# Two-part norms of a decoder stack: first products on four weight blocks, started inside the norm's first part

## The chip, the cores and the metric

One core of one Trainium2 chip runs the whole program. The metric is the device time of one execution in microseconds (us): the median of three runs, beside one more execution that was profiled.

Names used below: PE is TensorE (matrix products), DVE is VectorE, ACT is ScalarE, POOL is GpSimd, SP is SyncE, whose queue issues the weight loads. A norm here is an RMS norm. Everything is fp32; each operand of a large product is kept as a high part (h) and a rest (l), and a product is made of three: wh·xh, wh·xl and wl·xh.

## The reference, cut to what matters

Two stacks follow each other on 512 positions of width 1024, kept transposed as 8 tiles x[0..7] of 128 features by 512 positions. The first stack is two layers with norms ahead of each part. The second has two layers, each a mixer (an even one with attention and a state space, an odd one with a gated recurrence) and a feed-forward network, with a norm behind each part as well as ahead of it:

```
x = x + rmsnorm(mixer(rmsnorm(x, pre)), post)
x = x + rmsnorm(swiglu(rmsnorm(x, pre2)), post2)
swiglu(a) = (silu(a @ w_gate) * (a @ w_up)) @ w_down
```

So three times in the second stack a part ends with a norm behind it (a post norm, whose result is added to x) and the next norm ahead starts at once from the new x: even mixer to feed-forward network, feed-forward network to odd mixer, odd mixer to feed-forward network. The fourth post norm ends in the store of the output.

## The kernel before, in words

**Weights.** `plan` (L166) holds the list of all weight blocks in the order of use. `fill(n)` (L170) loads blocks ahead until n are waiting: a load into one of 3 `raw` buffers by SP's queue (L179), then wh on ACT (L181), then wl on DVE (L182), into 3 buffers each. `weights` (L185) fills to three and hands out the oldest. A full block is 128 by 1024 elements, 512 KB.

**Products.** `dense` (L200) makes a 128 by 512 output tile of one block: per 128 rows k three matmuls of 512 columns (L196 to L198). It can be told to do one half of the columns (`HALVES`, two slices of 256). `dense_first` (L209) is used for the first blocks behind a norm: it takes several blocks at once and makes first, for every k, wh·xh and wl·xh of each block (L218, L219), then wh·xl (L223), so that work on the first tiles can begin before the last are there. Behind a two-part norm it does so for columns 0 to 255 and then for 256 to 511.

**The two-part norm.** `PostNorm.last` (L1253) computes the last one or two output tiles of a part in two halves of the columns. The mean of squares is a product with a matrix of ones (L1251), of the sum of the earlier tiles' squares (`acc`, added up on POOL, L1237) and of each last tile's squares. Callbacks wait in `late` and are run by `flush` at given places in the last products. `finish(c)` (L1274) then makes rstd for the half (L239 to L242, two ACT and two DVE operations) and for each k scales y (L1279), subtracts it from x (L1280), and makes xn[k] h on ACT (`head`, L257); behind these come xn[k] l on DVE (`rest`, L261). After the second half `norm_square` (L264) squares each x tile on ACT and adds them on POOL (a copy for the first, L270, then 7 adds, L272); their sum feeds one product with the ones (L279) that gives the next norm's rstd, which is multiplied in only behind the products.

**Where it is used.** In the feed-forward networks behind a two-part norm, `dense_first` takes blocks 0 and 1 in halves, and blocks 2 and 3 follow as whole products (L307 to L309). In the odd mixer it takes blocks 0 to 2 in halves (L1851); block 3 follows as a whole one. The odd mixer goes on with a short convolution on DVE (`conv`, L1806), gates (`gates`, L1819) that need its split result (L532, L534), and further blocks named gb and xb.

**PSUM.** Each phase opens a pool of the 8 banks (`psums`, L147): in a feed-forward network 6 for products (`mm`) and 2 others, in the mixers 2 and 6, in the odd mixer 5 and 3. A phase's pool is given back at its end; the next phase's tiles wait for the old ones in the same bank.

**Order.** The program is written in one sequence; a planner then places each instruction on its engine's queue by its own estimate of when operands are ready, so neighbours on an engine can change places. Each engine then works its queue in order.

Of the kernel before, what the change touches and what calls it, by code (L numbers as in the profile page):

```python
# [9 lines left out]
F32 = mybir.dt.float32  # L10
FR = mybir.dt.float32r
# [7 lines left out]
S = 512  # L19
# [42 lines left out]
class Model:  # L62
    def __init__(self, tc, ap, ctx):
        self.tc, self.nc, self.ap, self.ctx = tc, tc.nc, ap, ctx
        nc = self.nc
        self.per = ctx.enter_context(tc.tile_pool(name="per", bufs=1))
        lead = self.per.tile([128, LEAD], F32, name="lead")
        nc.gpsimd.memset(lead, 0.0)
        self.act = ctx.enter_context(tc.tile_pool(name="act", bufs=1))
        self.wp = ctx.enter_context(tc.tile_pool(name="wp", bufs=1))  # L70
        self.tmp = ctx.enter_context(tc.tile_pool(name="tmp", bufs=2))
        self.dram = ctx.enter_context(tc.tile_pool(name="dram", bufs=1, space=bass.MemoryType.DRAM))
        self.x = []
# [72 lines left out]
    @contextmanager  # L146
    def psums(self, **bufs):  # L147

        with self.tc.tile_pool(name="ps", bufs=1, space=bass.MemoryType.PSUM, reuse_waits="tile") as p:
            self.ps, self.ps_bufs = p, bufs  # L150
            yield

    def psum(self, name, tag="px"):
        return self.ps.tile([128, S], F32, name=name, tag=tag, bufs=self.ps_bufs[tag])

# [14 lines left out]
    def fill(self, n):  # L170

        nc = self.nc
        while len(self.loaded) < n and self.todo:
# [5 lines left out]
            nc.sync.dma_start(raw, flat)  # L179
            h, l = (self.wp.tile([128, cols], FR, name=n, tag=n, bufs=3) for n in ("wh", "wl"))  # L180
            nc.scalar.activation(h, raw, AF.Copy)  # L181
# [18 lines left out]
    def dense(self, out, w, k0, nk, x, kt, c=slice(0, S), done=0):  # L200
# [3 lines left out]
        for k in range(done, nk):  # L204
            s = slice(k * 128, (k + 1) * 128)
            xh, xl = x[k0 + k]
            self.mm3(out[:, c], (h[:, s], l[:, s]), (xh[:, c], xl[:, c]), k0 + k == 0, k0 + k == kt - 1)

    def dense_first(self, srcs, name, parts):  # L209

        t = self.nc.tensor
        outs = [self.psum_mm(name) for w in srcs]
        ws = [self.weights(w) for w in srcs]
        for c in parts:
            for k in range(KD):
                s = slice(k * 128, (k + 1) * 128)
                for o, (h, l) in zip(outs, ws):
                    t.matmul(o[:, c], lhsT=h[:, s], rhs=self.xn[k][0][:, c], start=(k == 0), stop=False)  # L218
                    t.matmul(o[:, c], lhsT=l[:, s], rhs=self.xn[k][0][:, c], start=False, stop=False)  # L219
            for o, (h, l) in zip(outs, ws):  # L220
                for k in range(KD):
                    s = slice(k * 128, (k + 1) * 128)
                    t.matmul(o[:, c], lhsT=h[:, s], rhs=self.xn[k][1][:, c], start=False, stop=(k == KD - 1))  # L223
        return outs
# [38 lines left out]

    def norm_square(self, k):  # L264
        nc = self.nc
        sq = self.sq()
        nc.scalar.activation(sq, self.x[k], AF.Square)  # L267
        if self.sq_acc is None:
            self.sq_acc = self.tmp.tile([128, S], F32, name="sqacc", tag="sqacc", bufs=1)
            nc.gpsimd.tensor_copy(self.sq_acc, sq)  # L270
        else:
            nc.gpsimd.tensor_tensor(self.sq_acc, self.sq_acc, sq, op=ALU.add)  # L272

# [10 lines left out]
    def ffn(self, wgu, wd, out_tile, begin=None, side=None, pn=None):  # L284
# [3 lines left out]
        with tc.tile_pool(name="ffn", bufs=1, reuse_waits="tile") as hp, self.psums(mm=6, px=2):  # L288
# [7 lines left out]
            if pn:  # L296
                ready = self.dense_first([gu(i) for i in range(2)], "gu", HALVES)
            side = side(hp) if side else iter(())
# [7 lines left out]

            if pn:  # L307
                for i in (2, 3):
                    ready.append(gate_up(i))  # L309
            for m in range(KF):  # L310
# [35 lines left out]
LOOKAHEAD = 2  # L346
NRAW = 3
PARTS = ((0, 8), (8, 7), (15, 7))
HALVES = (slice(0, S // 2), slice(S // 2, S))
# [870 lines left out]
class PostNorm:  # L1220
# [32 lines left out]
    def last(self, tiles, x, kt):  # L1253
# [31 lines left out]
class NextNorm:  # L1285


    def __init__(self, M, gain):
# [17 lines left out]
class Store:  # L1306


    def __init__(self, M, out):
# [462 lines left out]
class Odd(Phase2):  # L1772
# [13 lines left out]
    def run(self, pn):  # L1786
        M, nc, tc = self.M, self.nc, self.tc
        act, tt, ts, stt = nc.scalar.activation, nc.vector.tensor_tensor, nc.vector.tensor_scalar, nc.vector.scalar_tensor_tensor
        with ExitStack() as st:
# [60 lines left out]

            ready = M.dense_first([self.ap["od_in"][i] for i in range(3)], "xb", HALVES)  # L1851
            conv(0)
# [85 lines left out]
```

## Time and profile before

| | |
|---|---|
| median of 3 runs | 3290.86 us (3290.36 to 3291.94) |
| the profiled execution's own time | 3292.49 us |
| its span, first to last instruction | 3290.7 us |
| mean granted TensorE clock | 0.991 |
| PE busy | 3200.9 us, 97% of the span |
| DVE, ACT, POOL busy | 1732.0, 1319.8, 187.2 us |
| even mixer to feed-forward network (called A) | about 2325 to 2385 us of the span |
| feed-forward network to odd mixer (B) | about 2708 to 2761 us |
| odd mixer to feed-forward network (C) | about 2885 to 2938 us |

How to read it: matmuls are pipelined, so the duration of one says less than the distance from its start to the next one's. The clock's two levels are 2.4 GHz (granted clock 1.0) and 1.2 GHz.

### The profile page before, as it was taken

The page shows a single profiled execution, that of the slowest core. Times are in us where ns is not written, and L with a number is a line of the kernel's source. Part 1 is how long each engine was busy: PE and PEld are TensorE (multiplying, and loading weights), DVE is VectorE, ACT ScalarE, POOL GpSimd, SP SyncE. Part 2 cuts the span into 40 slices and gives each one's busy share as a digit, 9 for nine tenths or more (in the row PEclk, how much of TensorE's full clock was granted, in tenths as well). Part 3 has the DMA queues.
Part 4 walks back from the last instruction along what each step waited for, and adds up shares of the span by engine and source line. Part 5 has one row for each costly group of instructions (what it writes and reads, how often), then busy time and mean ns, then how long its engine had stood idle before and what let it go on. Part 6 is the DMA issues. An engine that isn't in the chain of part 4 may idle for free.

```text
span 3290.7 us, 38872 instructions
## 1 busy us (share of the span) xinstructions
PE 3200.9 (97%) x15174; PEld 2566.7 (78%) x15178; DVE 1732.0 (53%) x2767; ACT 1319.8 (40%) x2041; POOL 187.2 (6%) x184
## 2 busy tenths in 40 slices
PE   8999999999999999999999999998999999989998
PEld 6888856788888888875778888876788887778887
DVE  5443468664433444357774443687554428664433
ACT  4232346743323332243763322355533227643322
POOL 1000100010000000010010000000200011010000
PEclk9999999999999999999999999999999999999999
DMA  4333341033333332343113333322233332323332
GB/s 158 111 97 97 108 128 61 26 107 100 97 94 100 96 96 93 100 126 98 49 62 96 96 93 100 113 79 58 93 96 96 93 100 71 102 71 96 97 95 79
DMA packets 114473, 306.65 MB, mean 93 GB/s; under 512 B 21840, under 2 KB 35056, under 8 KB 114288
## 3 DMA queue, kind: packets, MB, share of 16 engines
q1 hardware_dynamic: 114288, 304.16, 29.9%
q8 instruction: 119, 1.95, 0.2%
q14 instruction: 66, 0.54, 0.0%
HBM read 292.18 MB, written 10.09 MB: 92 GB/s over the span
## 4 chain that ended last, share of the span: by engine, by line
PE 86%; DVE 6%; ACT 4%; DMA 3%; issue 1%; SPq 0%; POOL 0%; DVEq 0%; ACTq 0%; POOLq 0%
PE gu L196 14%; PE gu L197 14%; PE gu L198 14%; PE o L197 8%; PE o L198 8%; PE o L196 8%; DMA conv<-hp_d 1%; PE conv L962 1%; PE wo L197 1%; PE wo L196 1%; PE wo L198 1%; PE lgD L1080 1%; PE v L196 1%; DVE wl L182 0%; PE v L197 0%
## 5 line engine op out<-in xcount | busy, mean ns | idle before, releaser
L181 ACT ACTIVATE wh<-raw 128x1024 fp32r<-128x1024 f32 (+2 forms) x550 | 550.3, 1001 | 1492.9 <-PE gu L197 843.0
L182 DVE TENSOR_TENSOR wl<-raw,wh 128x1024 fp32r<-128x1024 f32 (+2 forms) x550 | 633.0, 1151 | 547.3 <-ACT wh L181 542.7
L196 PE MATMUL o<-hid,wh 128*128 128x512 f32 (+1 forms) x1100 | 419.2, 381 | 0.0
L197 PE MATMUL o<-hid,wh 128*128 128x512 f32 (+1 forms) x1100 | 418.9, 381 | 0.0
L198 PE MATMUL o<-hid,wl 128*128 128x512 f32 (+1 forms) x1100 | 418.5, 380 | 0.0
L315 DVE SCALAR_TENSOR_TENSOR us<-gu,rstd 128x512 f32<-128x512 f32 x132 | 91.2, 691 | 400.7 <-PE gu L198 400.7
L196 PEld LDWEIGHTS o<-hid,wh 128*128 128x128 f32 x1100 | 206.8, 188 | 39.9
L197 PEld LDWEIGHTS o<-hid,wh 128*128 128x128 f32 x1100 | 206.8, 188 | 39.8
L198 PEld LDWEIGHTS o<-hid,wl 128*128 128x128 f32 x1100 | 206.8, 188 | 39.1
L313 DVE SCALAR_TENSOR_TENSOR gs<-gu,rstd 128x512 f32<-128x512 f32 x132 | 91.3, 692 | 259.3 <-PE gu L198 258.5
L272 POOL TENSOR_TENSOR sqacc<-sqacc,sq 128x512 f32<-128x512 f32 x70 | 104.2, 1488 | 369.4 <-ACT sq L267 367.4
L318 ACT ACTIVATE hid<-gs 128x512 fp32r<-128x512 f32 x132 | 83.5, 632 | 93.1 <-DVE gs L316 93.1
L196 PE MATMUL gu<-xn0h,wh 128*128 128x512 f32 x258 | 103.3, 400 | 0.0
L197 PE MATMUL gu<-xn6l,wh 128*128 128x512 f32 x258 | 100.6, 390 | 1.9 <-DVE xn6l L261 1.9
L197 PE MATMUL gu<-xn0l,wh 128*128 128x512 f32 x258 | 100.9, 391 | 0.0
L198 PE MATMUL gu<-xn0h,wl 128*128 128x512 f32 x258 | 100.9, 391 | 0.0
L198 PE MATMUL gu<-xn1h,wl 128*128 128x512 f32 x258 | 100.9, 391 | 0.0
L197 PE MATMUL gu<-xn1l,wh 128*128 128x512 f32 x258 | 100.9, 391 | 0.0
L197 PE MATMUL gu<-xn2l,wh 128*128 128x512 f32 x258 | 100.9, 391 | 0.0
L196 PE MATMUL gu<-xn1h,wh 128*128 128x512 f32 x258 | 100.9, 391 | 0.0
L196 PE MATMUL gu<-xn2h,wh 128*128 128x512 f32 x258 | 100.8, 391 | 0.0
L198 PE MATMUL gu<-xn2h,wl 128*128 128x512 f32 x258 | 100.7, 390 | 0.0
(1386 smaller groups left out, 7069.9 us busy)
## 6 DMA issues: line engine op xcount, KB each, us to landing
raw<-in_ffn_gu SPq DMA_DIRECT2D x176, 512.0 KB
raw<-in_f_gu SPq DMA_DIRECT2D x88, 512.0 KB
raw<-in_ffn_d SPq DMA_DIRECT2D x64, 448.0 KB
raw<-in_w_in SPq DMA_DIRECT2D x36, 512.0 KB
raw<-in_ffn_d SPq DMA_DIRECT2D x32, 512.0 KB
raw<-in_f_d SPq DMA_DIRECT2D x32, 448.0 KB
raw<-in_w_out SPq DMA_DIRECT2D x32, 256.0 KB
raw<-in_f_d SPq DMA_DIRECT2D x16, 512.0 KB
```

The lines of the kernel that those rows point to most:

```text
L181: nc.scalar.activation(h, raw, AF.Copy)
L182: nc.vector.tensor_tensor(l, raw, h.bitcast(F32), op=ALU.subtract)
L196: t.matmul(out, lhsT=wh, rhs=xh, start=first, stop=False)
L197: t.matmul(out, lhsT=wh, rhs=xl, start=False, stop=False)
L198: t.matmul(out, lhsT=wl, rhs=xh, start=False, stop=last)
L272: nc.gpsimd.tensor_tensor(self.sq_acc, self.sq_acc, sq, op=ALU.add)
L313: nc.vector.scalar_tensor_tensor(gs, g, -1.0, self.nrstd, op0=ALU.mult, op1=ALU.mult)
L315: nc.vector.scalar_tensor_tensor(us, u, -1.0, self.nrstd, op0=ALU.mult, op1=ALU.mult)
L318: nc.scalar.activation(h, gs, AF.Copy)
L962: nc.tensor.matmul(p[32 * g:32 * g + 32], lhsT=cw[:, g, k], rhs=st[:, g, 4 * k:4 * k + S], start=(k == 0), stop=(k == 7))
L1080: nc.tensor.matmul(lg[:, :C], lhsT=self.dq[h][:, q], rhs=self.dk[h][:, :C], start=True, stop=False)
```

## The change

Four edits go together.

- Two PSUM banks (`pp`) belong to no phase. In every phase they stand for two of the phase's mm banks, in rotation with the others, which begin with the third.
- `start_next`, called by `PostNorm.last` where another norm follows (three times, not at the store): behind the last product of the old part, the first blocks' wh·xh and wl·xh of columns 0 to 255 for k 0 to 3, for two blocks, into the two banks; then the flush that finishes the second half of the norm; then k 4 to 7.
- `dense_first` takes over what was started, and does four blocks in halves in all three places; wh and wl have 4 buffers each.
- The first half's xl (`rest`) is written behind the second half's rstd; the squares' sum starts on ACT directly, and the 7 adds behind a two-part norm go to DVE in place of POOL. With two last tiles, the first flush comes one tile later.

```diff
+        self.pp = ctx.enter_context(tc.tile_pool(name="pp", bufs=1, space=bass.MemoryType.PSUM, reuse_waits="tile"))
...
     def psum(self, name, tag="px"):
+        if tag == "mm":
+            self.turn = (self.turn + 1) % self.ps_bufs["mm"]
+            if self.turn < PP:
+                return self.pp.tile([128, S], F32, name=name, tag="pp", bufs=PP)
+            return self.ps.tile([128, S], F32, name=name, tag=tag, bufs=self.ps_bufs[tag] - PP)
...
-            h, l = (self.wp.tile([128, cols], FR, name=n, tag=n, bufs=3) for n in ("wh", "wl"))
+            h, l = (self.wp.tile([128, cols], FR, name=n, tag=n, bufs=NW2) for n in ("wh", "wl"))
...
+    def start_next(self, between):
+        self.fill(1 + LOOKAHEAD)
+        got = []
+        for i in range(2):
+            got.append(self.loaded.popleft())
+            self.fill(1 + LOOKAHEAD)
+        ws = [w for _, w in got]
+        outs = [self.pp.tile([128, S], F32, name="first", tag="pp", bufs=PP) for w in ws]
+        self.heads_first(outs, ws, HALVES[0], range(0, 4))
+        between()
+        self.heads_first(outs, ws, HALVES[0], range(4, KD))
+        self.started = outs, ws, [k for k, _ in got]
...
         for c in parts:
-            for k in range(KD):
-                s = slice(k * 128, (k + 1) * 128)
-                for o, (h, l) in zip(outs, ws):
-                    t.matmul(o[:, c], lhsT=h[:, s], rhs=self.xn[k][0][:, c], start=(k == 0), stop=False)
-                    t.matmul(o[:, c], lhsT=l[:, s], rhs=self.xn[k][0][:, c], start=False, stop=False)
+            if c.start or not n:
+                self.heads_first(outs, ws, c)
+            else:
+                self.heads_first(outs[n:], ws[n:], c)
...
-    def norm_square(self, k):
+    def norm_square(self, k, eng=None):
         nc = self.nc
+        if self.sq_acc is None:
+            self.sq_acc = self.tmp.tile([128, S], F32, name="sqacc", tag="sqacc", bufs=1)
+            nc.scalar.activation(self.sq_acc, self.x[k], AF.Square)
+            return
         sq = self.sq()
         nc.scalar.activation(sq, self.x[k], AF.Square)
-        if self.sq_acc is None:
-            self.sq_acc = self.tmp.tile([128, S], F32, name="sqacc", tag="sqacc", bufs=1)
-            nc.gpsimd.tensor_copy(self.sq_acc, sq)
-        else:
-            nc.gpsimd.tensor_tensor(self.sq_acc, self.sq_acc, sq, op=ALU.add)
+        (eng or nc.gpsimd).tensor_tensor(self.sq_acc, self.sq_acc, sq, op=ALU.add)
...
-                ready = self.dense_first([gu(i) for i in range(2)], "gu", HALVES)
+                ready = self.dense_first([gu(i) for i in range(4)], "gu", HALVES)
...
-                    if i == (len(parts) - 1 if c.start == 0 else 0):
+                    if c.start and i == 0 or c.start == 0 and m == KD - 1 and i == len(parts) - 1:
                         self.flush()
...
-        self.flush()
+        if self.next.follows:
+            self.M.start_next(self.flush)
+        else:
+            self.flush()
...
         r = M.rstd_of(self.ms[:, c])
+        if c.start:
+            self.next.rest(HALVES[0])
         for k in range(KD):
...
-        self.next.rest(c)
+        if c.start:
+            self.next.rest(c)
...
-                self.M.norm_square(k)
+                self.M.norm_square(k, self.M.nc.vector)
...
-            ready = M.dense_first([self.ap["od_in"][i] for i in range(3)], "xb", HALVES)
+            ready = M.dense_first([self.ap["od_in"][i] for i in range(4)], "xb", HALVES)
```

`PP` is 2 and `NW2` is 4. A scratch region for descriptors is halved to 1024 bytes.

## Rows read from the trace of the kernel before

**Rows 1.** The page: busy time of the engines over the whole span.

```profile
PE 3200.9 (97%) x15174; PEld 2566.7 (78%) x15178; DVE 1732.0 (53%) x2767; ACT 1319.8 (40%) x2041; POOL 187.2 (6%) x184
```

**Rows 2.** Stretches: length, busy of PE, PEld, DVE, ACT, POOL, clock, DMA share, GB/s.

```profile
2348.50:2385.30 36.80, 30.00 (x148) 24.01 (x147) 28.19 (x49) 16.11 (x32) 12.60 (x8) 0.86 0.20 70
2726.70:2760.50 33.80, 27.97 (x174) 24.95 (x174) 29.96 (x53) 20.40 (x34) 12.74 (x10) 0.90 0.25 82
2900.50:2937.80 37.30, 29.35 (x149) 24.62 (x148) 28.20 (x49) 16.16 (x31) 12.62 (x8) 0.86 0.21 69
2775.00:2815.00 40.00, 40.00 (x178) 33.12 (x177) 39.88 (x57) 38.11 (x50) 0.20 (x2) 1.00 0.36 113
```

**Rows 3.** Timeline of PE, neighbours in B and C: start, duration, what (idle before, and its releaser).

```profile
2729.79 0.28 PE L218 MATMUL xb<-xn0h,wh 128*128 128x256 f32 x1
2729.91 0.28 PE L219 MATMUL xb<-xn0h,wl 128*128 128x256 f32 x1
...
2907.20 0.41 PE L218 MATMUL gu<-xn2h,wh 128*128 128x256 f32 x1
2907.41 0.41 PE L219 MATMUL gu<-xn2h,wl 128*128 128x256 f32 x1
...
2935.04 0.39 PE L196 MATMUL gu<-xn4h,wh 128*128 128x512 f32 x1
2935.26 0.39 PE L197 MATMUL gu<-xn4l,wh 128*128 128x512 f32 x1
```

**Rows 4.** Timeline of PE around C: matmuls that waited.

```profile
2888.53 0.70 PE L1251 MATMUL ms<-sqacc,ones 128*128 128x256 f32 x2 [1.27 <-POOL sqacc L1237]
...
2902.79 0.70 PE L1251 MATMUL ms<-sq,ones 128*128 128x256 f32 x2 [2.10 <-ACT sq L1231]
...
2905.75 0.58 PE L218 MATMUL gu<-xn0h,wh 128*128 128x256 f32 x1 [2.03 <-DVE sq L241]
...
2919.75 0.38 PE L223 MATMUL gu<-xn3l,wh 128*128 128x256 f32 x1 [0.91 <-DVE xn3l L261]
```

**Rows 5.** Timelines of ACT, DVE and POOL around C.

```profile
2899.54 0.51 ACT L257 ACTIVATE xn0h<-x,vecs 128x256 fp32r<-128x256 f32 x1 [1.27 <-DVE x L1280]
...
2905.40 0.49 ACT L257 ACTIVATE xn7h<-x,vecs 128x256 fp32r<-128x256 f32 x1
...
2906.01 0.48 DVE L261 SCALAR_TENSOR_TENSOR xn1l<-x,vecs,xn1h 128x256 fp32r<-128x256 f32 x1
...
2909.23 0.76 DVE L1279 TENSOR_TENSOR pn<-pn,rstd 128x256 f32<-128x256 f32 x2
...
2915.24 9.84 POOL L272 TENSOR_TENSOR sqacc<-sqacc,sq 128x512 f32<-128x512 f32 x7
...
2918.21 1.49 DVE L261 SCALAR_TENSOR_TENSOR xn3l<-x,vecs,xn3h 128x256 fp32r<-128x256 f32 x1
...
2943.17 0.69 DVE L316 TENSOR_TENSOR gs<-gs,us 128x512 f32<-128x512 f32 x1
```

**Rows 6.** Timelines of ACT and DVE: the weight splits behind C's first products.

```profile
2926.04 2.00 ACT L181 ACTIVATE wh<-raw 128x1024 fp32r<-128x1024 f32 x2 [3.12 <-PE gu L223]
...
2933.38 1.23 DVE L182 TENSOR_TENSOR wl<-raw,wh 128x1024 fp32r<-128x1024 f32 x1 [3.89 <-ACT wh L181]
```

**Rows 7.** Timeline of PE in B: the mean, the ones product, the block behind it.

```profile
2729.02 0.70 PE L1251 MATMUL ms<-sq,ones 128*128 128x256 f32 x2 [2.10 <-ACT sq L1231]
...
2753.26 1.91 PE L279 MATMUL ms<-sqacc,ones 128*128 128x512 f32 x2
2754.18 1.27 PE L196 MATMUL xb<-xn0h,wh 128*128 128x512 f32 x1
...
2760.53 0.39 PE L196 MATMUL gb<-xn0h,wh 128*128 128x512 f32 x1
```

**Rows 8.** The odd mixer's last gates: DVE's split and PE's first gate product.

```profile
2814.10 0.69 DVE L534 TENSOR_TENSOR sl<-xc,sh 128x512 fp32r<-128x512 f32 x1
...
2816.00 0.39 PE L196 MATMUL gate<-sh,wh 128*128 128x512 f32 x1
```

More of the change, by code (lines that the diff above doesn't have):

```diff
@@ L72, in __init__ @@
         self.dram = ctx.enter_context(tc.tile_pool(name="dram", bufs=1, space=bass.MemoryType.DRAM))
+        self.pp = ctx.enter_context(tc.tile_pool(name="pp", bufs=1, space=bass.MemoryType.PSUM, reuse_waits="tile"))
+        self.turn = 0
+        self.started = None
         self.x = []
@@ L149, in psums @@
         with self.tc.tile_pool(name="ps", bufs=1, space=bass.MemoryType.PSUM, reuse_waits="tile") as p:
-            self.ps, self.ps_bufs = p, bufs
+            self.ps, self.ps_bufs, self.turn = p, bufs, 1
             yield
     def psum(self, name, tag="px"):
+        if tag == "mm":
[3 more added lines that the diff above has]
+            return self.ps.tile([128, S], F32, name=name, tag=tag, bufs=self.ps_bufs[tag] - PP)
         return self.ps.tile([128, S], F32, name=name, tag=tag, bufs=self.ps_bufs[tag])
@@ L207, in dense, with heads_first @@
             self.mm3(out[:, c], (h[:, s], l[:, s]), (xh[:, c], xl[:, c]), k0 + k == 0, k0 + k == kt - 1)
+    def heads_first(self, outs, ws, c, ks=range(KD)):
+        t = self.nc.tensor
+        for k in ks:
+            s = slice(k * 128, (k + 1) * 128)
+            for o, (h, l) in zip(outs, ws):
+                t.matmul(o[:, c], lhsT=h[:, s], rhs=self.xn[k][0][:, c], start=(k == 0), stop=False)
+                t.matmul(o[:, c], lhsT=l[:, s], rhs=self.xn[k][0][:, c], start=False, stop=False)
+    def start_next(self, between):
[10 more added lines that the diff above has]
+        self.started = outs, ws, [k for k, _ in got]
     def dense_first(self, srcs, name, parts):
         t = self.nc.tensor
-        outs = [self.psum_mm(name) for w in srcs]
-        ws = [self.weights(w) for w in srcs]
-        for c in parts:
-            for k in range(KD):
-                s = slice(k * 128, (k + 1) * 128)
-                for o, (h, l) in zip(outs, ws):
-                    t.matmul(o[:, c], lhsT=h[:, s], rhs=self.xn[k][0][:, c], start=(k == 0), stop=False)
-                    t.matmul(o[:, c], lhsT=l[:, s], rhs=self.xn[k][0][:, c], start=False, stop=False)
+        outs, ws, n = [], [], 0
+        if self.started:
+            outs, ws, keys = self.started
+            n, self.started = len(outs), None
+            for key, src in zip(keys, srcs):
+                assert key.tensor is src.tensor and key.offset == src.offset, (key, src)
+        while len(outs) < len(srcs):
+            ws.append(self.weights(srcs[len(outs)]))
+            outs.append(self.psum_mm(name))
+        for c in parts:
+            if c.start or not n:
+                self.heads_first(outs, ws, c)
+            else:
+                self.heads_first(outs[n:], ws[n:], c)
             for o, (h, l) in zip(outs, ws):
@@ L305, in gate_up @@
                 return o
-            if pn:
-                for i in (2, 3):
-                    ready.append(gate_up(i))
             for m in range(KF):
@@ L347 @@
 NRAW = 3
+NW2 = 4
+PP = 2
 PARTS = ((0, 8), (8, 7), (15, 7))
@@ L1281, in finish @@
             self.next.head(k, c)
-        self.next.rest(c)
+        if c.start:
+            self.next.rest(c)
 class NextNorm:
+    follows = True
     def __init__(self, M, gain):
@@ L1302, in rest @@
             for k in range(KD):
-                self.M.norm_square(k)
+                self.M.norm_square(k, self.M.nc.vector)
 class Store:
+    follows = False
     def __init__(self, M, out):
@@ L1928 @@
     P = host_pack(I)
-    nc = bacc.Bacc("TRN2", target_bir_lowering=False, num_devices=1, dynamic_dma_scratch_size=2048)
+    nc = bacc.Bacc("TRN2", target_bir_lowering=False, num_devices=1, dynamic_dma_scratch_size=1024)
     ap = {n: nc.dram_tensor("in_" + n, a.shape, mybir.dt.from_np(a.dtype), kind="ExternalInput").ap()
```

## The prediction

> **What bounds the kernel now.** I read the page first: PE is busy 97% of the span [rows 1], so the matmul stream sets the end, and a change pays only where that stream stands still or runs slowly. Then the stretches around the three places where one norm follows another. In A, B and C the granted clock is 0.86 to 0.90 and PE is busy for 30.0 of 36.8, 28.0 of 33.8 and 29.4 of 37.3 us [rows 2]; the reader should see that these 108 us hold both idle time and slow time. Each stretch runs from the end of the old part's last product to the end of the new part's fourth block (B: with the ones product).
>
> Third, the distances between matmul starts, because durations overlap: 0.12 us for 256 columns and 0.225 for 512 at the full clock, 0.21 for 256 at the lower level [rows 3]. Last, PE's waits in C [rows 4]: 1.27 for POOL's sum, 2.10 for ACT's square of the last tile, 2.03 for a DVE read of the means (the new product's bank is the one that the means lay in), then about 0.9 per step for xn l. Behind the second long wait about twelve matmuls run at 1.2 GHz (the second pair of [rows 3]); in B, behind a single one of 2.10, they run at 0.12 at once (the first pair of [rows 3]). A has the first, second and last kinds, B the second and last.
>
> Why are the xn l late? DVE makes one in 0.48 us, 0.40 from start to start, while POOL rests, and in 1.49 while POOL adds squares (7 adds in 9.84, 1.41 each) [rows 5]. The two proceed in step, so PE is fed at POOL's pace.
>
> **The change, part by part (C as the worked case).**
>
> *PE's own work from the old part's end to the fourth block's end.* One mean, charged with its full 0.70 [rows 4], and 4 blocks × 8 k × 3 products × 2 halves = 192 half matmuls × 0.12 = 23.0. Blocks 2 and 3 in halves cost 96 × 0.12 - 48 × 0.225 = 0.7 more than whole; that is inside the 23.0.
>
> *What is left of the gap.* The last xn h of the first half starts at 2905.40 and takes 0.49 [rows 5], 5.4 after the old part's end at 2900.5. Its chain (means, rstd, y, x, head, with two weight splits between) has the same members after the change and shifts with PE, so it stays 5.4. PE has the mean and 32 half matmuls of two blocks to do by then, 4.5 us, and the last four (0.5) must come behind that xn h: 5.4 + 0.5 - 4.5 = 1.4 us idle at most. If the planner draws blocks 2 and 3 forward, it is nil. I take 1.3, since the program has them last. The second half's mean now stands behind 16 of these products on PE's queue (1.9 us), and the rstd on ACT and DVE behind it; DVE is still on the first half's x by then, so nil. Sum 0.7 + 23.0 + 1.3 = 25.0 against 37.3: **12.3 saved**.
>
> *Does DVE keep up?* Behind the first half's x it owes rstd 0.9 (two operations like the 0.48 one), eight xl at 0.40 (3.2), sixteen y and x operations in pairs of 0.67 by start spacing (5.4), eight xl (3.2), seven adds (0.69 each [rows 5], 4.3 to 4.8): 17.0 to 17.5 us. PE meanwhile has 7.7 us of the first half left (blocks 2 and 3, then xl of all four), then 7.7 of xh and 3.8 of xl for the second. The first second-half xn h comes after 0.9 + 3.2 + 1.3 + about 0.8 on ACT (head 0.51 and what it waits) = 6.2, needed at 7.7; the last xl at 12.7, needed from 15.4; the sum at 17.5, needed at 19.2. All are covered, by 1.5 us at the least. If that cover goes, the same wait returns piece by piece.
>
> *Adds on DVE.* With POOL's adds kept, the eight second-half xl would take 8 × 1.41 = 11.3 and end at 20.8, some 4.5 us after PE wants the last of them for its first block. The move is therefore worth about 4.5 per norm within the 12.3, and costs DVE about 4.5 us in time it has. The Trainium skill (Perfetto Trace Analysis, Optimizing Scalar/DVE Operations) says that moving work between GPSIMD and DVE may not help, since they share a read port; the 0.48 against 1.49 shows the sharing, but says the move does help here. By that rule alone the sum would be some 13 us poorer. The first square written straight into the sum saves a copy on POOL, which nothing waits for then: nil.
>
> *Later first flush.* The 1.27 for POOL [rows 4] goes: the mean of the sum is now asked 12 half matmuls after the next tile began, that is 2.9 us later. C: another 1.3.
>
> *Fourth weight buffers, and the loads.* Four blocks are held until their wh·xl of the second half. Block 4 is split only when block 0 is let go, as ACT now waits 3.12 for it [rows 6]; then come about 1.0 on ACT and 1.23 on DVE, 2.3 in all, while PE has 24 × 0.12 = 2.9 left on the other three. Cost nil with 0.6 to spare; without that cover up to 2.3 per place. Two more loads of 512 KB are issued early on SP; DMA engines are busy 20 to 25% in these stretches [rows 2], so nil, and nothing waits behind them. The smaller descriptor scratch touches none of these loads: nil.
>
> *Two fixed banks.* They remove the 2.03 wait in C and the slow matmuls behind it (in the 12.3 already). The other phases keep their number of banks: nil. A planner that reorders elsewhere is the unknown; I bound it by one wait of the size seen here, 2 us either way.
>
> *A.* Same as C: 36.8 - 25.0 = 11.8, and the same POOL wait of 1.27: **13.1**. C: 12.3 + 1.3 = **13.6**.
>
> *B.* One last tile, so no POOL wait to remove. Its mean is fed at 2729.02 [rows 7], 2.3 behind the old end, and ACT made that square behind its last xn h; 16 of the new products (1.9) fit ahead of it, so 0.4 stays idle. New run: 0.7 + 23.0 + 0.4 = 24.1, then the ones product. That product started 2753.26 [rows 7], 26.6 into the stretch; it now starts at 24.1. PE ends four blocks and the ones product (0.9 to the next start) at 25.0 in place of 33.8 and is **8.8 ahead**. But the odd mixer is then fed by DVE: DVE is busy 39.9 of 40 us [rows 2], and its last split ends at 2814.8, 1.2 before PE's gates use it [rows 8]. DVE's row of work starts at the rstd, only 2.5 earlier, and is one weight split (1.2) shorter, since block 3 was split before. So PE can keep 2.5 + 1.2 + 1.2 = **4.9** of the 8.8; between 2.5 and 8.8.
>
> Sum: 13.1 + 13.6 + 4.9 = 31.6. Against the profiled execution (3292.49) that is 3260.9; the median of the runs shown lies 1.6 below it, so **3259 us**.
>
> **The rivals.**
>
> 1. *The odd mixer keeps all.* PE does later blocks while it waits for gates, and B gives 8.8. For it: PE's order is planned, and later blocks need no DVE result. Against: weight blocks come in a fixed order, with the gates' blocks between. 31.6 + 3.9 = 35.5, with the 1.3 idle of A and C gone 38: 3253 to 3255. Chance 0.17.
>
> 2. *The adds gain nothing on DVE*: put between the xl in place of behind them, they delay these as POOL did. 3 × 4.5 lost: 3272. Against: they come last in the program. Chance 0.08. The Trainium skill's sentence above (Perfetto Trace Analysis, Optimizing Scalar/DVE Operations) would end here.
>
> 3. *The next split becomes the wait.* Block 4's split comes late by its 2.3 in all three places, and 2 us idle remain in the first half, after which twelve or so matmuls run at 0.21: 3 × (2.3 + 2 + 1.1) = 16: 3275. For it: 0.6 us of cover is thin. Chance 0.10.
>
> 4. *Nothing is started early*: the planner puts the first products behind the finish as now. The bank wait and POOL's pace still go; each place keeps about 2.1: 3266, inside my range. Chance 0.06.
>
> 5. *Slower: the clock.* Place: the 192 half matmuls. If PE is fed in drops, one xn h each 0.4 to 1 us, the clock falls as behind the waits in C and stays at 1.2 GHz through all of them: 3 × 192 × (0.21 - 0.12) = 52, so 3259 + 52 = 3311, 20 slower than now. It decides only if over 117 of the 192 run slow in each place (31.6 / 3 / 0.09); about twelve did so in C behind two waits, none in B behind one [rows 3]. The Trainium skill (TensorE: Matmul & The Clock Gate, Part 1) says that the throttled state is the default and activity releases it; by that the drops would be the risk. Chance 0.03.
>
> 6. *The planner moves what I did not read*, in the phases between, by as much as is gained: no row speaks for it. Chance 0.06, five parts in six of it for no difference.
>
> **How the numbers follow.** Forecast 0.50, rivals 0.17, 0.08, 0.10, 0.06, 0.03 and 0.06. The likeliest is 3259. The range reaches to rival 1 with the unknown 2 us and some more idle removed (3247) and to rival 3 (3275). What a measurement of this kernel can tell from no change is 0.2%, 6.6 us; the forecast and rivals 1 to 4 pass it by far, so faster is 0.50 + 0.17 + 0.08 + 0.10 + 0.06 = 0.91. No difference is 0.05, slower 0.03 + 0.01 = 0.04.
>
> **What would show it.** Right: behind the old part's last product PE goes on at 0.12 with the new blocks, the waits for ACT's square and the means' bank are gone; xn l in 0.40 steps in both halves, no POOL adds there; about 25 us to the fourth block in A and C; clock near 1.0 in those stretches; in the odd mixer new PE waits for gates' operands, some 4 us. Wrong: waits for wh or wl behind the fourth block, 0.21 steps, or B's gain kept whole.

## The result and the profile after

The changed kernel takes 3250.29 us (median of 4 runs, 3250.12 to 3252.71); the kernel before took 3291.40 beside it (4 runs, 3290.36 to 3291.97). The ratio is 0.9877, interval [0.9860, 0.9894]: 41 us faster, where 32 were forecast. The profiled execution took 3250.12 us with a span of 3248.3.

The page of the changed kernel, the busy row that answers to [rows 1]:

```profile
PE 3179.6 (98%) x15294; PEld 2560.3 (79%) x15298; DVE 1719.9 (53%) x2788; ACT 1314.0 (40%) x2040; POOL 151.6 (5%) x153
```

PE is still the bound; its busy time too is 21 us shorter. Now the stretches that answer to [rows 2]: each from the end of the old part's last product to the end of the new part's fourth block, for A, B and C, and then 40 us of the odd mixer (length; PE, PEld, DVE, ACT, POOL; clock, DMA share, GB/s):

```profile
2336.80:2361.20 24.40, 23.93 (x197) 23.57 (x196) 23.28 (x54) 15.69 (x30) 0.00 (x0) 1.00 0.12 40
2702.60:2726.30 23.70, 23.70 (x197) 23.50 (x196) 21.54 (x54) 17.35 (x31) 0.14 (x2) 1.00 0.15 49
2871.00:2895.40 24.40, 23.93 (x197) 23.57 (x196) 23.27 (x54) 15.67 (x30) 0.00 (x0) 1.00 0.12 41
2745.00:2785.00 40.00, 37.05 (x156) 29.72 (x155) 39.76 (x56) 36.14 (x48) 0.40 (x4) 0.96 0.33 105
```

24.4, 23.7 and 24.4 us stand in place of 36.8, 33.8 and 37.3, at a granted clock of 1.00 in place of 0.86 to 0.90. (B's 33.8 held the ones product too; with it B takes 24.1, from 2702.60 to the next product at 2726.72.) The timeline of PE at the seam of A shows why (start, duration, what, idle before and its releaser):

```profile
2336.68 0.28 PE L207 MATMUL o<-sh,wl 128*128 128x256 f32 x1
2336.80 0.28 PE L224 MATMUL first<-xn0h,wh 128*128 128x256 f32 x1
...
2338.38 0.39 PE L224 MATMUL first<-xn2h,wh 128*128 128x256 f32 x1 [0.47 <-ACT xn2h L296]
2338.61 0.28 PE L225 MATMUL first<-xn2h,wl 128*128 128x256 f32 x1
...
2340.04 0.60 PE L1289 MATMUL ms<-sq,ones 128*128 128x256 f32 x2
...
2361.16 1.02 PE L318 MATMUL ms<-sqacc,ones 128*128 128x512 f32 x2
2361.62 0.79 PE L205 MATMUL gu<-xn0h,wh 128*128 128x512 f32 x1
```

The new products follow the old ones at 0.12, one wait of 0.47 is left, and the mean of the second half (L1289) waits for nothing: the 2.10 and 2.03 of [rows 4] are gone. The fifth block (L205) begins right behind the ones product; no split is late here. The timeline of DVE in C, second half, answers to [rows 5]:

```profile
2884.67 0.48 DVE L300 SCALAR_TENSOR_TENSOR xn0l<-x,vecs,xn0h 128x256 fp32r<-128x256 f32 x1
2885.07 0.47 DVE L300 SCALAR_TENSOR_TENSOR xn1l<-x,vecs,xn1h 128x256 fp32r<-128x256 f32 x1
...
2887.44 0.48 DVE L300 SCALAR_TENSOR_TENSOR xn7l<-x,vecs,xn7h 128x256 fp32r<-128x256 f32 x1
2887.84 5.39 DVE L311 TENSOR_TENSOR sqacc<-sqacc,sq 128x512 f32<-128x512 f32 x7
```

Eight xn l in 0.40 steps where they took 1.4 each, then seven adds in 5.39.

The two traces were then cut at the same seven events. Each number is the distance between the starts (at the squares: the ends) of two rows of one trace: the eighth square ahead of the first mixer, the eighth square ahead of the even mixer, DVE's last ssm product of the even mixer, the ones product behind A, B's first mean, the odd mixer's last split on ACT, the ones product behind C, the end.

| us | before | after | saved | forecast |
|---|---|---|---|---|
| first network | 380.7 | 382.7 | -2.0 | 0 |
| rest of the first stack | 1706.7 | 1696.1 | 10.6 | 0 |
| even mixer up to A | 213.2 | 211.7 | 1.5 | 0 |
| A | 84.7 | 70.7 | 14.0 | 13.1 |
| network between | 330.1 | 330.0 | 0.1 | 0 |
| B and the odd mixer | 140.0 | 136.2 | 3.8 | 4.9 |
| last parts and C | 82.4 | 68.0 | 14.4 | 13.6 |
| to the end | 353.0 | 353.0 | 0 | 0 |

The three places give 32.2 against 31.6 forecast. The surplus is in the first stack, where no two-part norm stands; the first network takes 2.0 of it back. (The even mixer's 1.5 is less than what this stretch differs by from one execution to another, 211.5 to 214.1 in the traces of the changed kernel's order.)

### The profile page after: what moved, and what is told of

Read it like the earlier page. It is cut to its first block, busy times and chain, and to the rows that moved or that the text cites. A ratio compares the mean times of both kernels' runs of the same rounds, so it can differ in the third digit from the quotient of the medians.

```text
span 3248.3 us, 39097 instructions
## 1 busy us (share of the span) xinstructions
PE 3179.6 (98%) x15294; PEld 2560.3 (79%) x15298; DVE 1719.9 (53%) x2788; ACT 1314.0 (40%) x2040; POOL 151.6 (5%) x153
## 4 chain that ended last, share of the span: by engine, by line
PE 88%; ACT 4%; DVE 4%; DMA 2%; issue 1%; SPq 0%; POOL 0%; DVEq 0%; ACTq 0%
PE gu L206 14%; PE gu L205 14%; PE gu L207 14%; PE o L206 8%; PE o L205 8%; PE o L207 8%; DMA conv<-hp_d 2%; PE conv L1000 1%; PE wo L206 1%; PE wo L205 1%; PE wo L207 1%; PE v L207 1%; PE v L206 1%; PE v L205 1%; ACT gAqb L886 0%
## 5 line engine op out<-in xcount | busy, mean ns | idle before, releaser
L205 PE MATMUL o<-hid,wh 128*128 128x512 f32 (+1 forms) x1100 | 419.2, 381 | 0.0
L205 PEld LDWEIGHTS o<-hid,wh 128*128 128x128 f32 x1100 | 206.8, 188 | 39.6
L311 POOL TENSOR_TENSOR sqacc<-sqacc,sq 128x512 f32<-128x512 f32 x49 | 82.8, 1690 | 1580.6 <-ACT sq L310 1540.6
L205 PE MATMUL gu<-xn0h,wh 128*128 128x512 f32 x254 | 101.3, 399 | 0.0
L352 DVE TENSOR_TENSOR gs<-gs,us 128x512 f32<-128x512 f32 x132 | 91.3, 692 | 15.7 <-ACT gs L350 3.8
L205 PE MATMUL gu<-xn1h,wh 128*128 128x512 f32 x254 | 98.8, 389 | 0.0
L205 PE MATMUL gu<-xn7h,wh 128*128 128x512 f32 x254 | 98.8, 389 | 0.0
```

The costliest lines, as they stand in the source:

```text
L205: t.matmul(out, lhsT=wh, rhs=xh, start=first, stop=False)
L311: (eng or nc.gpsimd).tensor_tensor(self.sq_acc, self.sq_acc, sq, op=ALU.add)
L352: nc.vector.tensor_tensor(gs, gs, us, op=ALU.mult)
```

## The experiments

The same cuts through every run's trace (first network, first stack, A, B and odd mixer, C), beside its median and its ratio to the kernel before:

| run | first network | first stack | A | B, odd | C | median us | ratio, interval |
|---|---|---|---|---|---|---|---|
| b_nw4 | 383.1 | 1696.1 | 86.5 | 138.5 | 84.2 | 3285.61 | 0.9983 [0.9974, 0.9992] |
| b_pp | 380.4 | 1702.5 | 84.7 | 140.0 | 82.4 | 3290.60 | 0.9999 [0.9990, 1.0008] |
| a_again | 383.0 | 1695.4 | 70.8 | 136.6 | 68.0 | 3252.03 | 0.9890 [0.9875, 0.9904] |
| a_nostart | 386.3 | 1696.8 | 76.4 | 140.2 | 70.4 | 3264.76 | 0.9920 [0.9906, 0.9935] |
| a_pool | 382.2 | 1698.4 | 75.1 | 138.0 | 72.4 | 3263.45 | 0.9915 [0.9898, 0.9932] |
| a_2blocks | 383.7 | 1696.0 | 73.8 | 133.4 | 71.9 | 3256.35 | 0.9903 [0.9886, 0.9919] |
| a_flush | 384.4 | 1695.1 | 72.2 | 138.3 | 69.5 | 3257.39 | 0.9906 [0.9892, 0.9921] |
| a_nw3 | 382.6 | 1709.0 | 72.4 | 139.6 | 69.6 | 3265.02 | 0.9914 [0.9897, 0.9930] |
| a_begdve | 378.6 | 1695.4 | 70.8 | 136.5 | 68.0 | 3247.16 | 0.9875 [0.9860, 0.9890] |
| a_odd3 | 378.6 | 1696.8 | 70.7 | 133.6 | 68.0 | 3245.28 | 0.9858 [0.9841, 0.9874] |
| a_odd2 | 378.0 | 1694.9 | 70.7 | 135.9 | 67.7 | 3247.79 | 0.9863 [0.9849, 0.9878] |

### Four weight buffers alone, and the fixed banks alone

Run b_nw4, against the kernel before:

```diff
-            h, l = (self.wp.tile([128, cols], FR, name=n, tag=n, bufs=3) for n in ("wh", "wl"))
+            h, l = (self.wp.tile([128, cols], FR, name=n, tag=n, bufs=4) for n in ("wh", "wl"))
...
-    nc = bacc.Bacc(..., dynamic_dma_scratch_size=2048)
+    nc = bacc.Bacc(..., dynamic_dma_scratch_size=1024)
```

> The kernel before with four buffers each for wh and wl in place of three, and the smaller descriptor scratch; nothing else. Open: the first stack's two mixers gained 5.7 and 5.0 us in the changed kernel and the even mixer some 1.5, and the first 40 us lost 1.9; the forecast had nil for all of them. Theory 1 (the fourth buffer lets splits of later blocks be made sooner, so the mixers' blocks come in another order): the gains and the loss are here alone, 10 us gained by the end of the second mixer less 1.9, the stretches A, B and C unchanged in length: 3291 - 10 = about 3281 us. Theory 2 (the fixed banks do it): the mixers are as before, within 0.5 us each: 3291 us. Theory 3 (the planner's order follows from all edits together): a gain that matches neither, anywhere from 3285 to 3297.

Run b_pp, against the kernel before (the pool `pp` and the start of `turn` as in the change):

```diff
     def psum(self, name, tag="px"):
+        if tag == "mm":
+            self.turn = (self.turn + 1) % self.ps_bufs["mm"]
+            if self.turn < PP:
+                return self.pp.tile([128, S], F32, name=name, tag="pp", bufs=PP)
+            return self.ps.tile([128, S], F32, name=name, tag=tag, bufs=self.ps_bufs[tag] - PP)
```

> The kernel before with the two fixed PSUM banks and their rotation; nothing else. Theory 2 (the banks make the mixers faster): 10 us gained by the end of the second mixer. On top of it, under every theory, the wait of about 2.0 us for the bank of the means in B and C may shrink, as the new product's tiles no longer follow those of the phase in which the means lay; with the slow matmuls behind it that is at most 3 us per place, and nil if the rotation gives the same bank. Theory 2: 3275 to 3281 us. Theory 1 (the fourth weight buffer did it): 3285 to 3291. The loss of 1.9 in the first 40 us is here if the banks' rotation there makes it, and not if the buffers do.

Measured: the buffers alone make the first stack 1696.1, the length that it has in the changed kernel, and the first network 2.4 longer. But A and C get 1.8 longer each, so the median is only 5.9 lower (3291.56 for the kernel before beside it), and 3285.6 stands above the 3281 of theory 1. Part of what the norms lose shows in ACT's order. The timeline of ACT in C, before:

```profile
2901.98 0.49 ACT L257 ACTIVATE xn3h<-x,vecs 128x256 fp32r<-128x256 f32 x1
2902.38 0.36 ACT L1231 ACTIVATE sq<-o 128x256 f32<-128x256 f32 x1
```

and in b_nw4, with the mean on PE behind it:

```profile
2893.60 0.49 ACT L257 ACTIVATE xn5h<-x,vecs 128x256 fp32r<-128x256 f32 x1
2894.00 0.36 ACT L1231 ACTIVATE sq<-o 128x256 f32<-128x256 f32 x1
2894.41 1.22 PE L1251 MATMUL ms<-sq,ones 128*128 128x256 f32 x2 [2.89 <-ACT sq L1231]
```

The planner puts the last tile's square behind two xn h more (xn4h and xn5h, 0.40 each), and the mean waits 2.89 in place of 2.10; in C the second block's first product then waits 3.38 for the bank of the means, where it was 2.03. The first half's last xn h, in turn, ends 4.2 us behind the old part, where it was 5.4 before. The changed kernel has this order too.

The banks alone change nothing that the timing can tell; A, B and C keep their lengths to 0.1. But this run doesn't say what a free bank is worth: the rotation begins with the phase's own banks, so the first products don't get the fixed ones, and the wait for the bank of the means is still there in C:

```profile
2899.86 0.58 PE L225 MATMUL gu<-xn0h,wh 128*128 128x256 f32 x1 [2.03 <-DVE sq L248]
```

The first stack is 1702.5 there with the order of instructions of the kernel before (the two orders first differ at 2090 us), so some 4 us of its length is variation between executions. That weakens one profile's 10.6, hence the reverse test below.

### Back to three buffers

Run a_nw3, against the changed kernel (the odd mixer's range likewise; the fourth block follows whole):

```diff
-NW2 = 4
+NW2 = 3
...
-ready = self.dense_first([gu(i) for i in range(4)], "gu", HALVES)
+ready = self.dense_first([gu(i) for i in range(3)], "gu", HALVES)
```

> The changed kernel with three buffers each for wh and wl again, so dense_first takes three blocks in all three places and the fourth follows whole; banks, early start, adds on DVE and the later flush stay. Theory 1 (the fourth buffer makes the first stack's mixers faster): from the end of the first network to the end of the first stack 1702 to 1707 us again, as in the two profiles with three buffers (1706.7 and 1702.5), in place of 1695 to 1698 as in the eight with four, and the first network's end sooner, near 380.5 us in place of 382 to 386. The three places: three blocks behind the networks' norms cover less than four and more than two: 0 to 3 us each in A and C; from B to C, B's first mean to C's first mean 167 to 171. Sum 3250 + 8.5 - 2.5 + 0 to 4: 3255 to 3261 us. Rival (the first stack's gain came from the banks or the straight first square): 1695 to 1698 stays, 3247 to 3253 us. Rival (with three buffers the splits of the held blocks stop everything behind them): A and C fall back by 5 and more, 3265 and more.

Measured: the first stack is 1709.0. Over all traces: three buffers 1702.5, 1706.7 and 1709.0, four buffers 1694.9 to 1698.4 in ten. The groups don't overlap and their means lie 10.0 apart: the fourth buffer is the cause, shown in both directions. (The descriptor scratch, which b_nw4 changed with it, stays halved here, so it is not the scratch.) A and C lose 1.6 each, inside what was expected. The odd mixer loses 3.0 to 3.4, which was not: B's first mean to C's takes 173.6 us, where 167 to 171 were expected, and the median of 3265.0 lies above the 3255 to 3261 of theory 1. The first network did not return to 380.5, so as far as one trace can say, its loss is not the buffers' alone.

How a buffer shortens a mixer can be read in part, though no run prices it wait by wait. The timeline of ACT in the second mixer of the kernel before (columns as above):

```profile
1455.63 0.59 ACT L1022 ACTIVATE uk<-uk 128x512 f32<-128x512 f32 x1
1457.15 0.38 ACT L1035 ACTIVATE dv<-uv 128x256 f32<-128x256 f32 x1 [0.93 <-PE uv L198]
1458.24 0.38 ACT L1035 ACTIVATE dv<-uv 128x256 f32<-128x256 f32 x1 [0.71 <-PE uv L198]
```

The timeline of PE there:

```profile
1457.59 0.38 PE L196 MATMUL uv<-wh,sh 128*128 128x256 f32 x1 [0.47 <-ACT dv L1035]
1458.68 0.38 PE L196 MATMUL uv<-wh,sh 128*128 128x256 f32 x1 [0.47 <-ACT dv L1035]
...
1460.86 0.49 PE L196 MATMUL cu<-xn0h,wh 128*128 128x512 f32 x1 [0.47 <-DMA iqs<-iq_d]
```

The window of 11 us around it (columns as in the windows above), before:

```profile
1455.00:1466.00 11.00, 8.36 (x34) 6.62 (x34) 5.35 (x9) 7.21 (x17) 1.22 (x3) 0.84 0.70 177
```

and after, laid at the same uk product:

```profile
1451.00:1462.00 11.00, 9.80 (x48) 7.55 (x47) 3.36 (x5) 5.82 (x14) 1.45 (x3) 1.00 0.95 222
```

PE and ACT hand the narrow uv tiles back and forth one at a time, PE falls idle for 0.47 again and again, and the granted clock of these 11 us is 0.84: the next block (cu) begins in steps of 0.43, where 0.23 is the full clock's. With the fourth buffer the planner's order differs: PE starts 48 matmuls in place of 34 in the 11 us, at the full clock.

### The early start taken away

Run a_nostart, against the changed kernel:

```diff
         if self.next.follows:
-            self.M.start_next(self.flush)
+            self.flush()
```

> The changed kernel with the products of the first two blocks no longer written ahead of the second half's finish: the flush stands alone there, as before, and dense_first makes all four blocks itself. Forecast: the second half's mean is then again the first thing on the tensor engine behind the old part, and it waits 2.10 us for the square of the last tile as in the kernel before in all three places; a few slow matmuls behind it: 2.1 to 3.4 per place, of which the odd mixer may give back its part: 3250 + 4 to 3250 + 10, middle 3257. Rival (the planner brings the first products forward by itself, since the xn of the first half are there): no difference, 3250. Rival (the whole of the twelve us per place hangs on the early start): 3250 + 25 and more.

Measured: 12.7 slower than the changed kernel's own second timing (a_again, on another chip; by the two ratios 10, against its first timing 14.5); A +5.7, B and odd mixer +3.6 to 4.0, C +2.4. The median lies above the 3254 to 3260 expected. The timeline of PE in A:

```profile
2344.05 1.22 PE L1289 MATMUL ms<-sq,ones 128*128 128x256 f32 x2 [2.89 <-ACT sq L1269]
2344.71 0.78 PE L224 MATMUL gu<-xn0h,wh 128*128 128x256 f32 x1
2345.28 0.42 PE L225 MATMUL gu<-xn0h,wl 128*128 128x256 f32 x1
2345.50 0.42 PE L224 MATMUL gu<-xn0h,wh 128*128 128x256 f32 x1
...
2346.87 0.58 PE L224 MATMUL gu<-xn0h,wh 128*128 128x256 f32 x1 [0.74 <-DVE sq L280]
```

and in C:

```profile
2887.96 0.70 PE L1289 MATMUL ms<-sq,ones 128*128 128x256 f32 x2 [2.89 <-ACT sq L1269]
...
2888.62 0.28 PE L225 MATMUL gu<-xn0h,wl 128*128 128x256 f32 x1
2888.74 0.28 PE L224 MATMUL gu<-xn0h,wh 128*128 128x256 f32 x1
```

The mean waits for ACT's square again, for 2.89 as in b_nw4 and not the 2.10 that the expectation took. In A the matmuls behind go at 0.21, the lower clock, and a second wait of 0.74, for the bank of the means, follows. In C the same wait of 2.89 is followed by steps of 0.12, and there is no second wait; what decides whether the clock falls is not shown. So a place pays 2.4 for the wait alone and 5.7 with the slow matmuls and the second wait. The planner did not bring the products forward by itself.

### The adds back on POOL

Run a_pool, against the changed kernel:

```diff
-                self.M.norm_square(k, self.M.nc.vector)
+                self.M.norm_square(k)
```

> The changed kernel with the seven adds of squares on POOL, as in the kernel before (the first square still goes straight into the sum). Forecast: they slow DVE's xn l of the second half from 0.40 to 1.41 each, the last of them comes 4.5 us late: 3250 + 3 x 4.5 = about 3263 us, a little less where the odd mixer is fed by DVE anyway (3259 to 3264). Rival (the adds don't matter where four blocks cover them: the xn l are needed late enough): 3250 to 3252. Rival (POOL's adds, 9.8 us from the first square on, end behind the four blocks, and the ones product waits for them too): 3265 to 3275.

Measured: 3263.45, as forecast: A +4.3, C +4.4, B and the odd mixer +1.4 to 1.8. The timeline of DVE in C, second half:

```profile
2895.34 1.52 DVE L300 SCALAR_TENSOR_TENSOR xn1l<-x,vecs,xn1h 128x256 fp32r<-128x256 f32 x1
...
2902.50 1.48 DVE L300 SCALAR_TENSOR_TENSOR xn6l<-x,vecs,xn6h 128x256 fp32r<-128x256 f32 x1
2903.91 0.47 DVE L300 SCALAR_TENSOR_TENSOR xn7l<-x,vecs,xn7h 128x256 fp32r<-128x256 f32 x1
```

and that of POOL:

```profile
2892.57 11.14 POOL L311 TENSOR_TENSOR sqacc<-sqacc,sq 128x512 f32<-128x512 f32 x7 [22.82 <-ACT sq L310]
```

The xn l take 1.5 while POOL adds and 0.47 the moment it stops.

### Two blocks in place of four; the first flush where it was

Run a_2blocks, against the changed kernel (in the odd mixer three in place of four; blocks 2 and 3 of the networks follow whole):

```diff
-ready = self.dense_first([gu(i) for i in range(4)], "gu", HALVES)
+ready = self.dense_first([gu(i) for i in range(2)], "gu", HALVES)
```

> The changed kernel with dense_first on two blocks behind a two-part norm in the feed-forward networks (three in the odd mixer), as before; blocks 2 and 3 follow whole. Early start, banks, adds on DVE, four buffers stay. Forecast: PE has 7.7 us of work in two blocks behind the first half's last xn h (xl of the first half 1.9, xh of the second 3.8, its xl 1.9), while DVE's last xl of the second half comes 12.7 to 13.2 us behind that point: 5.0 to 5.5 idle per place, less the 0.7 that whole blocks save: 4.3 to 4.8 in A and C each, and in B, with three blocks (11.5 us of work), 1.2 to 1.7, of which the odd mixer gives back a part. Sum 9 to 11: 3259 to 3262 us. Rival (the early start and the faster xn l are enough, blocks 2 and 3 cover nothing): 3249 to 3251. Rival (as without the early start, each place falls back by all it gained): 3275 and more.

Run a_flush, against the changed kernel:

```diff
-if c.start and i == 0 or c.start == 0 and m == KD - 1 and i == len(parts) - 1:
+if i == (len(parts) - 1 if c.start == 0 else 0):
```

> The changed kernel with the first flush where it was: behind the first part-column of every last tile, not of the last alone. Forecast: the wait for POOL's sum returns in A and C, 1.27 each: 3250 + 2.5 = 3252.8 us, the mean's ones product again first behind the tile before; B as it is. Rival (the later flush costs what it saves, since the first half's finish starts 2.9 us later and the first xn h with it): 3248 to 3250, the first half's last xn h nearer to the old part's end and the remaining 0.6 us of idle time at xn2h gone.

The changed kernel itself a second time, run a_again:

> The changed kernel itself, for its spread on the chip on which the next three run: 3250 to 3253 us, and in its trace the same order of instructions; the waits for the convolution's loads in the two first mixers and the first 40 us may differ by some us from those of the first profile (two kernels that share its order up to 2290 us differed by 1.2 and 2.8 us in the first mixer, and by 3.6 in the first 40 us).

Measured with two blocks: A +3.1, C +3.9, a little under the 4.3 to 4.8. In the timeline of PE in C the tensor engine outruns the second half's first xn h:

```profile
2881.93 0.50 PE L262 MATMUL first<-xn7l,wh 128*128 128x256 f32 x2
2883.48 0.48 PE L224 MATMUL first<-xn0h,wh 128*128 128x256 f32 x1 [1.04 <-ACT xn0h L296]
2883.75 0.42 PE L225 MATMUL first<-xn0h,wl 128*128 128x256 f32 x1
```

But B and the odd mixer got 3 us *shorter*, on the other side of what was expected (1.2 to 1.7 longer, in part given back), and the median of 3256.4 is below the 3259 to 3262 expected. Four blocks may be one too many there; two more runs follow that up.

With the old flush, A and C are each 1.5 longer; POOL's sum is waited for 1.3 in both, as before. The median is 5.4 above that of a_again, 2.4 more than these two give and above the 3252.8 expected. In this one profile 1.4 stands in the first network, where executions of one and the same order differ by more (382.2 to 386.3), and 1.7 in the odd mixer, where ACT's order is unchanged: not settled, and no part of the claim.

### Two edits further: the first norm's adds on DVE, fewer blocks in the odd mixer

Run a_begdve, against the changed kernel, in `begin`:

```diff
             for k in range(KD):
-                M.norm_square(k)
+                M.norm_square(k, nc.vector)
```

> The changed kernel with the first norm's adds (at the very start) on DVE too. In the changed kernel ACT's squares there wait for POOL's adds (0.44 us each, six times) and the xn h behind them on ACT are late; PE waits 2.2 us for POOL's sum. Theory (POOL's pace is what the start lost): the sum comes 2 to 3 us sooner, hid0.1 at 38 to 39 us in place of 41.3, and 3248 us. Rival (the start waits for loads and for the weight splits; DVE's adds then delay wl or xn l by 0.69 each): no change, 3250 to 3252. Rival (worse): DVE, with splits and xn l to do, brings the sum later than POOL: 3252 to 3255.

Measured: 3247.16 (3246.83 to 3248.39) against 3252.03 (3251.21 to 3253.42) for the changed kernel on the same chip; the first network ends at 378.6 in place of 383.0. The timeline of ACT at the start of the changed kernel:

```profile
12.71 0.63 ACT L310 ACTIVATE sq<-x 128x512 f32<-128x512 f32 x1 [0.83 <-POOL sqacc L311]
13.25 0.71 ACT L296 ACTIVATE xn3h<-x,vecs 128x512 fp32r<-128x512 f32 x1
14.40 0.64 ACT L310 ACTIVATE sq<-x 128x512 f32<-128x512 f32 x1 [0.44 <-POOL sqacc L311]
14.94 0.71 ACT L296 ACTIVATE xn4h<-x,vecs 128x512 fp32r<-128x512 f32 x1
```

and with the adds on DVE:

```profile
12.24 0.71 ACT L296 ACTIVATE xn3h<-x,vecs 128x512 fp32r<-128x512 f32 x1
12.86 0.61 ACT L310 ACTIVATE sq<-x 128x512 f32<-128x512 f32 x1
13.37 0.71 ACT L296 ACTIVATE xn4h<-x,vecs 128x512 fp32r<-128x512 f32 x1
```

In the changed kernel a square stands ahead of each xn h on ACT and waits for POOL to free its buffer, so the xn h come every 1.69 us (POOL's pace). In the kernel before, the planner had them ahead of the squares, 0.61 apart. PE then waits 2.2 for POOL's sum, about as long as before the change (2.4). With DVE's adds both waits are gone.

Run a_odd3, against a_begdve (run a_odd2 has 2 there):

```diff
-ready = M.dense_first([self.ap["od_in"][i] for i in range(4)], "xb", HALVES)
+ready = M.dense_first([self.ap["od_in"][i] for i in range(3)], "xb", HALVES)
```

> The changed kernel with two more edits: the first norm's adds on DVE (the run before this one with that edit alone: 3247.2 us), and the odd mixer's first products on three blocks in place of four. Theory (four blocks hold all four weight buffers there, so the splits of the gates' blocks and of the next ones come late, PE waits some 2.5 us for a split and runs slowly behind it; in the run with two and three blocks B and the odd mixer together were 3.1 us shorter, 167.4 against 170.5 us): the same 3 us here, A and C unchanged: 3244 us, B's first mean to C's first mean 167 to 168 us. Rival (those 3 us came from elsewhere in that run, from the whole blocks 2 and 3 of the networks around it): B's first mean to C's first mean stays 170 to 171, 3247 us.

> As the run with three blocks in the odd mixer, with two there. Theory (fewer blocks free buffers sooner, but PE outruns the norm: two blocks cost the networks 3.1 and 3.9 us in A and C): B's own run is 3 to 4 us longer than with three, of which the odd mixer, which DVE feeds, takes back most or all: 3244 to 3247 us, B's first mean to C's first mean 167.5 to 170. Rival (buffers are all that counts): another 1 to 3 us shorter, 3241 to 3243. Rival (PE's lead is what counts): 3247 to 3250.

Measured: with three blocks B and the odd mixer take 133.6 in place of 136.5, the 3 us of the theory; with two, 135.9, and a median of 3247.8, just above the 3244 to 3247 expected. The median with three is 3245.28, ratio 0.9858; the intervals of a_begdve and a_odd3 overlap, so that step rests on the traces of this stretch, which repeats to 0.4 in the changed kernel. With three it is the fastest version run: 47 us below the kernel before (3245.28 against 3292.49). The timeline of PE in the odd mixer of the changed kernel, with four blocks:

```profile
2766.71 0.39 PE L207 MATMUL xb<-xn7h,wl 128*128 128x512 f32 x1
2769.58 0.79 PE L205 MATMUL xb<-xn0h,wh 128*128 128x512 f32 x1 [2.48 <-ACT wh L190]
2770.17 0.63 PE L206 MATMUL xb<-xn0l,wh 128*128 128x512 f32 x1
2770.60 0.73 PE L205 MATMUL gate<-sh,wh 128*128 128x512 f32 x1
```

PE comes early and then waits 2.48 for a weight split, with 0.43 steps behind it. The timeline of ACT ahead of this split:

```profile
2766.14 1.28 ACT L1891 ACT_TABLE_LOAD   x1
2767.43 1.15 ACT L1891 ACTIVATE gr<-gr 128x512 f32<-128x512 f32 x2
2768.49 2.94 ACT L190 ACTIVATE wh<-raw 128x1024 fp32r<-128x1024 f32 x3
```

The profile shows no idle time of ACT here: the split stands on its queue behind the gates' operations and three table loads of 1.28 us between 2761 and 2767.5. So it was ACT's queue, and not a full buffer, that PE waited for at that moment. That held buffers delay this split is the theory that foresaw the 3 us; whether they do it by way of the planner's order is not shown. With three blocks a wait of 2.3 for a split is still there, at a later block, so the wait moved and the whole got shorter. Which of ACT's operations sets it was not tried.

## Why the prediction was right, and where it was off

**The places.** 32.2 saved against 31.6. A and C gave 14.0 and 14.4 against 13.1 and 13.6: the run to the fourth block is 24.4, not 25.0, since PE stands still for 0.6 and not 1.3. The prediction let the last xn h of the first half stay "5.4" behind the old part's end, with "the same members" in its chain; it ends there at 4.2, as in b_nw4, since the fourth buffer changed ACT's order. POOL's wait at the first flush is worth 1.5 with its return (forecast 1.27 to 1.3). Taken away one at a time, the early start, the adds on DVE, the blocks beyond two and the later flush cost A 5.7, 4.3, 3.1 and 1.5, together about 14.5 where 14.0 were gained, and C 2.4, 4.4, 3.9 and 1.5, together about 12.2 of 14.4. The share of the fixed banks by themselves was not measured.

**The odd mixer.** PE ended B 9.7 ahead (24.1 against 33.8; forecast 8.8), and 3.8 were kept, against 4.9. The reason held in part: DVE is busy 39.76 of 40 us. But the prediction had PE wait for gates' operands, "some 4 us", and the trace has 0.2 of that; the new waits are the 2.48 for ACT's weight split and 1.4 that the profile puts down to DVE's read of an earlier xb product (zp). That the three places meet the forecast to 0.6 is in part luck: A and C lay 1.7 above it, B 1.1 below. The count of blocks was a part not foreseen; "one weight split shorter, since block 3 was split before" was booked as a gain for four blocks, and three give 3 us more.

**The step that failed** is the cost of the fourth weight buffers: the prediction asked only whether the held blocks' splits come late ("Cost nil with 0.6 to spare") and bounded everything elsewhere by "one wait of the size seen here, 2 us either way". Measured: about 10 us in the first stack's two mixers, which the buffers alone give and three buffers take away. Without them, by subtraction, the time would have been some 3260, near the forecast; by the time alone, 3250.3 is nearer to rival 1's 3253 to 3255, whose reason failed. In the same way "The first square written straight into the sum ... nil" overlooked the norm at the start, where squares and xn h share ACT and the squares wait for POOL's adds. The first network is 1.4 to 5.6 us longer in the traces with four buffers and POOL's adds, 1.9 in a_nw3 with three; which edit does how much of it stays open, and DVE's adds take it away.

**The rivals.** Rival 1 fell, as 3.8 of B's lead were kept. Rivals 2 and 3 fell: the adds come behind the last xl, and the fifth block starts at once. Rival 6, the planner moving what was not read, happened, but with the other sign: it gained. Moving the adds was forecast at 4.5 per norm; 4.3 and 4.4 came out in A and C. The Trainium skill (Perfetto Trace Analysis, Optimizing Scalar/DVE Operations) says that work moved between these two engines may gain nothing for their shared port; here it gains 11.4 by the medians (3263.45 against 3252.03, on two chips; 8 by the ratios) and 10.1 to 10.5 by the three places, since beside POOL's adds DVE's xn l take three times their length. Rival 4 gave 3266 as the time with nothing started early; taken away, it is 3264.8, but that agreement is luck: the rival let each place keep 2.1 above 3259, and the run shows 2.4 to 5.7 a place above 3250 to 3252. Rival 5, the clock, fell: 1.00 in all three stretches, with one wait of 0.47 in each of A and C. The Trainium skill (TensorE: Matmul & The Clock Gate, Part 1) takes the throttled state for the default, which activity releases; the traces agree in so far as the wait of 2.89 in A of a_nostart brings 0.21 back, but in C of the same run the same wait is followed by 0.12.

## What to carry to other kernels

An extra buffer for a stream that runs through the whole program changes the order everywhere: cost it in the phases that the edit was not made for, and look there for stretches in which PE is idle in short steps at a lowered clock. Where one engine's row of operations stretches another's threefold, as POOL's adds did to DVE's xn l here, it is worth moving onto the slowed engine itself, if it can come behind them. The number of blocks held over a wait is to be tried per place (of those run, four were best in A and C, three in the odd mixer): enough to cover the norm, but, as the three blocks in the odd mixer suggest, not all the buffers where the next phase waits for splits.

## What the runs showed of the hardware

Not expected: how much executions with the same order differ. Kernels that agree instruction for instruction up to 2290 us (after, a_nostart, a_pool) needed 307.4, 308.6 and 310.2 us for the first mixer, and their first networks ended at 382.7, 386.3 and 382.2. In the mixers PE waits about 6 us for the convolution's loads in each trace, most of it in steps of up to 2.8. A single profile is therefore no measure for gains of 2 to 4 us there; A, C and the networks behind them repeat to 0.1 in the changed kernel.
